# Where split weights stand in their buffers: one fixed place, or 64 places in turn

## The chip, the cores and the metric

One Trainium2 chip, of which the kernel uses one core. The metric is device time in microseconds (us) of one execution of the whole program; smaller is better. Times of several executions are given as a median with the lowest and the highest.

## What is computed

One step of a decoder layer for a prompt group (256 tokens) and a sample group (8 sequences of 4 tokens), served with the same weights. With D_MODEL = 2048 and D_FF = 8192, the reference comes down to

```python
h = rms_norm(x, g_mix)
u_lin, u_gate, q_sb, k_sb, v_sb, q_mem, gate_logits = split(h @ w_in)
y_conv = silu(layer_norm(depthwise_causal_conv(u_lin * sigmoid(u_gate)))) @ w_conv_out
y_sb   = stick_breaking_attention(rms_norm(q_sb), rms_norm(k_sb), v_sb) @ w_sb_out
y_mem  = softmax_attention(rms_norm(q_mem), mem_k, mem_v) @ w_mem_out
g      = sigmoid(gate_logits + b_gate)            # three gates of D_MODEL each
x = x + (g[0]*y_conv + g[1]*y_sb + g[2]*y_mem) @ w_o
x = x + square(relu(rms_norm(x, g_mlp) @ w_up)) @ w_down
```

All data are float32. Keys, values and convolution history are returned as well. Nearly all of the arithmetic is in the products with the weight matrices, which are some 264 MB and are each used for all 288 tokens at once.

## The kernel before, in words

**Precision.** A float32 product is made of three products in the one-pass type F32R. Each operand is split into a high part (a rounded copy) and a low part (what is left), and weight and activation are multiplied as high by high, high by low and low by high.

**Slabs.** All weights lie in `wall`, cut in the order of use into 504 slabs of 128 partitions by 1,024 numbers (`SLAB`), that is, 8 blocks of 128 by 128. For each slab four steps follow each other:

1. SP issues the load into one of four `wr` buffers (`load_slab`, the DMA on L283).
2. ScalarE casts it to the high part, in one of four `wh` buffers (`cast_weights`, L305).
3. VectorE subtracts, which gives the low part, in one of four `wl` buffers (`sub_part`, L316).
4. TensorE uses it: `products` (L494) makes 24 matmuls out of a full slab, 8 blocks by three products, all issued by `chunk` on L488.

In each matmul on L488 the stationary operand (the weights that TensorE loads) is a block of 128 columns of a `wh` or `wl` buffer. The moving operand is an activation tile of 288 columns, and the result is added up in a PSUM bank.

**The first 16 slabs** (for the memory's keys and values, `mem_products`) are used the other way round: the slab is the moving operand, 512 columns at a time, and a block of an activation is the stationary one (L541). They are loaded and split in two halves of 512.

**Places.** `wh` and `wl` tiles have 1,088 numbers in a partition, 64 (`PAD`) more than a slab needs. `shifted` (L286 to L288) returns the part of such a tile that begins at a given number of elements:

```python
    def shifted(p, s):
        n = 0 if s < 2 * KT // 2 else SHIFT
        return tl(p, [P, SLAB + PAD], F32R)[:, n:n + SLAB]
```

`KT` is 16, so slabs 0 to 15 begin at 0 and slabs 16 to 503 at `SHIFT`, which is 5. L305 and L316 write the part that it returned and L488 reads blocks of it.

The moving tiles have places of their own. The class `Acts` (L325) takes tiles of 320 numbers (`APART`) from the pool `a` and begins 4 (`AHEAD`) in, or 32 for the memory's tokens. `make_homes` (L1243) cuts buffers of the pools `k4` and `s` into tiles that begin 36 (`HOME`) in, or 36 plus a multiple of 320. By the addresses of the built program, counted in 4-byte words modulo 64, this comes to the following: every moving tile of L488 begins at word 60, every block of weights on L488 at word 29, and on L541 both operands at word 24. Of the small products with operands of their own, L853 to L855 (attention scores and values, 256 columns or 128) have stationary operands at word 56 and moving ones at 56 or 24, and L827 (sums of squares for a head, 288 columns, stationary operand `ones_r`) has them at 8 and at 24 or 56. L1107 to L1109 and L908 are transposes.

**Order.** The order of the work is made by a small planner in the kernel (the class `Order`), with a generator for each job and estimated costs. It decides on each engine what comes next from those costs, buffers that come free, and ranks. The place of a slab enters none of its numbers.

Of the kernel before, what the change touches and what calls it, by code (L numbers as in the profile page):

```python
# [16 lines left out]
KT = D_MODEL // P  # L17
# [156 lines left out]
APART = 320  # L174
AHEAD, HOME = 4, 36
PAD = 64
SHIFT = 5
VISIT, VISIT_K = 4, 8
MM = 0.131
MM_MEM = 0.226  # L180
# [3 lines left out]
def tile_decoder_step(ctx: ExitStack, tc: tile.TileContext, xT, memT, wall, cvec, kmat, ptab,  # L184
# [23 lines left out]
    def tl(p, shape, dt=F32):  # L208
        cnt[0] += 1
        return pools[p].tile(shape, dt, tag=p, name=f"{p}_{cnt[0]}")  # L210
# [73 lines left out]
        sl.landed[part].at = order.landed(n * P * 4 / 1e3)  # L284

    def shifted(p, s):  # L286
        n = 0 if s < 2 * KT // 2 else SHIFT
        return tl(p, [P, SLAB + PAD], F32R)[:, n:n + SLAB]  # L288

    def due(s):  # L290
# [4 lines left out]
    def cast_weights():  # L295
        todo = [(0, 0), (1, 0), (0, 1), (1, 1)] + [(s, i) for s in range(2, N_SLABS) for i in range(slabs[s].parts)]
        for s, i in todo:
            sl = slabs[s]
            n = SLAB // sl.parts
            cast_at[0] = s  # L300
            yield act(n, sl.landed[i], **({} if i else {"w": 1}))
            if i == 0:
                sl.h = shifted("wh", s)
            c = slice(i * n, (i + 1) * n)
            nc.scalar.copy(sl.h[:, c], sl.raw[:, c])  # L305
            sl.split[i].cast = order.now.ready
            add(sub_part(s, i), lambda s=s: 0 if due(s) - order.free["DVE"] < 5.0 else 4.5)

    def sub_part(s, i):
        sl = slabs[s]  # L310
        n = SLAB // sl.parts
        yield dve(n, late=Order.HOP + 0.1)
        if i == 0:
            sl.l = shifted("wl", s)
        c = slice(i * n, (i + 1) * n)
        nc.vector.tensor_sub(sl.l[:, c], sl.raw[:, c], sl.h[:, c].bitcast(F32))  # L316
        done(sl.split[i])
        if i == sl.parts - 1:
            give("wr")
# [1301 lines left out]
```

## Time and profile before

| what | value |
| --- | --- |
| median of 2 runs | 1635.16 us (1635.15 to 1635.18) |
| profiled execution, span from first to last instruction | 1632.5 us |
| TensorE busy, share of the span | 1627.7 us, 100% |
| VectorE busy | 992.1 us, 61% |
| ScalarE busy | 739.3 us, 45% |
| GpSimd busy | 139.1 us, 9% |
| HBM read, written | 297.05 MB, 6.32 MB |
| matmuls | 12,786, of which 11,712 on L488 |

The profiled execution's own time is its span, 1632.5 us, and what lies around it: the median of the runs is 2.7 us more than the span. Rows name an engine (PE is TensorE's matmuls, PEld its weight loads, DVE VectorE, ACT ScalarE, POOL GpSimd, SP the queue that issues DMAs), a line of the kernel, an operation, and tiles as result<-operands. "Who waited for whom" gives idle time of an engine by what ended it. The chain of waits is followed back from the last instruction, and shows what the end of the program hangs on; its pieces have a start, a length, a line and a count. In the windows each engine's busy time stands for a stretch of time, with the granted TensorE clock as a share of full speed. Matmuls overlap each other, so the time that a stream of them takes is read from the distance of their starts, not from the busy time of one.

### The profile page before, as it was taken

To read this page: it belongs to the slowest core of one execution; us is meant where nothing else is said; L and a number is where in the kernel's file an instruction comes from. 1 tells how busy PE (TensorE), PEld (TensorE's weight loads), DVE (VectorE), ACT (ScalarE), POOL (GpSimd) and SP (SyncE) were. 2 spreads that over 40 slices of the span, in tenths; PEclk is the share of its full clock that TensorE was granted. 3 is DMA by queue.
4 is the path that set the end of the run, shared out by engine and by line. 5 is a ranking of instruction groups with operands and counts; after the bars stand their busy time and mean duration, and the time that the engine had idled before them with its cause. 6 is when DMAs were issued, how large, how long until landed. Compare 5 with 4: busy or idle time off the path is not lost.

```text
span 1632.5 us, 30962 instructions
## 1 busy us (share of the span) xinstructions
PE 1627.7 (100%) x12786; PEld 1610.3 (99%) x12786; DVE 992.1 (61%) x1471; ACT 739.3 (45%) x1070; POOL 139.1 (9%) x104
## 2 busy tenths in 40 slices
PE   9999999999999999999999999999999999999999
PEld 7999999999999999999999999999999999999999
DVE  8889888877677655565555544455445554455443
ACT  8746766644444534444443333333333333333332
POOL 0020000000000000001222200121001210022100
PEclk9999999999999999999999999999999999999999
DMA  9787465777755555546655555555555555555563
GB/s 339 217 186 251 153 209 189 248 257 252 254 166 169 163 179 167 174 153 212 191 176 168 169 168 168 169 169 174 165 173 170 168 170 169 168 168 168 180 194 99
DMA packets 107103, 305.39 MB, mean 187 GB/s; under 512 B 19922, under 2 KB 29522, under 8 KB 106962
## 3 DMA queue, kind: packets, MB, share of 16 engines
q1 hardware_dynamic: 106818, 303.39, 58.2%
q8 instruction: 100, 1.64, 0.4%
q14 instruction: 41, 0.34, 0.1%
q10 hardware_dynamic: 144, 0.02, 0.0%
HBM read 297.05 MB, written 6.32 MB: 186 GB/s over the span
## 4 chain that ended last, share of the span: by engine, by line
PE 99%; DMA 0%; SPq 0%; ACT 0%; DVE 0%; issue 0%
PE pm L488 93%; PE pm L541 3%; PE pa L488 1%; PE pl L1017 1%; PE pl L1190 0%; PE pa L854 0%; PE pa L855 0%; PE pa L853 0%; DMA wr<-in_wall 0%; PE pl L1033 0%; PE pa L827 0%; PE pa L1144 0%; PE pa L908 0%; PE pa L1141 0%; PE pa L1143 0%; PE pa L1107 0%
## 5 line engine op out<-in xcount | busy, mean ns | idle before, releaser
L305 ACT CAST wh<-wr 128x1024 fp32r<-128x1024 f32 (+1 forms) x520 | 530.3, 1022 | 648.1 <-PE pm L488 597.0
L488 PE MATMUL pm<-a,wh 128*128 128x288 f32 x5184 | 739.1, 293 | 0.0
L316 DVE TENSOR_TENSOR wl<-wr,wh 128x1024 fp32r<-128x1024 f32 (+1 forms) x520 | 617.2, 1190 | 195.2 <-ACT wh L305 190.5
L488 PEld LDWEIGHTS pm<-a,wh 128*128 128x128 f32 x5184 | 696.7, 188 | 1.3 <-issue 1.2
L488 PE MATMUL pm<-a,wl 128*128 128x288 f32 x2592 | 397.0, 292 | 0.0
L488 PEld LDWEIGHTS pm<-a,wl 128*128 128x128 f32 x2592 | 358.4, 188 | 0.0
L488 PE MATMUL pm<-k,wh 128*128 128x288 f32 x2160 | 306.7, 292 | 0.0
L488 PEld LDWEIGHTS pm<-k,wh 128*128 128x128 f32 x2160 | 290.2, 188 | 0.0
L488 PE MATMUL pm<-k,wl 128*128 128x288 f32 x1120 | 171.6, 292 | 0.0
L488 PEld LDWEIGHTS pm<-k,wl 128*128 128x128 f32 x1120 | 155.1, 188 | 0.0
L1346 POOL TENSOR_TENSOR t<-t 128x288 f32<-128x288 f32 x64 | 96.7, 1511 | 599.5 <-DVE t L1343 599.5
L1360 DVE TENSOR_TENSOR a<-a,pm 128x288 f32<-128x288 f32 x64 | 29.0, 454 | 122.4 <-PE pm L488 122.4
L1343 DVE SCALAR_TENSOR_TENSOR t<-pm,rx 128x288 f32<-128x288 f32 x64 | 29.2, 457 | 90.4 <-PE pm L488 90.4
L1349 ACT CAST k<-t 128x288 fp32r<-128x288 f32 x56 | 24.1, 433 | 115.6 <-POOL t L1346 115.6
L1262 DVE TENSOR_TENSOR t<-pm,rx 128x288 f32<-128x288 f32 x48 | 22.0, 458 | 71.5 <-PE pm L488 71.5
L488 PE MATMUL pm<-s,wh 128*128 128x288 f32 x400 | 65.1, 292 | 0.0
L719 DVE SCALAR_TENSOR_TENSOR a<-a,cv,a 128x256 f32<-128x256 f32 x120 | 57.5, 480 | 1.4
L1332 POOL TENSOR_TENSOR t<-t,t 128x288 f32<-128x288 f32 x15 | 21.6, 1441 | 419.3 <-ACT t L1329 419.3
L488 PEld LDWEIGHTS pm<-s,wh 128*128 128x128 f32 x400 | 56.6, 188 | 0.0
L1351 DVE TENSOR_TENSOR k<-t,k 128x288 fp32r<-128x288 f32 x52 | 23.8, 458 | 51.1 <-ACT k L1349 51.1
L541 PE MATMUL pm<-wh,a 128*128 128x512 f32 x128 | 34.6, 391 | 0.2 <-ACT wh L305 0.2
L488 PE MATMUL pm<-s,wl 128*128 128x288 f32 x160 | 33.8, 292 | 0.0
(212 smaller groups left out, 784.4 us busy)
## 6 DMA issues: line engine op xcount, KB each, us to landing
wr<-in_wall SPq DMA_DIRECT2D x488, 512.0 KB, 3.6
wr<-in_wall SPq DMA_DIRECT2D x32, 256.0 KB, 4.8
k<-in_kpool SPq DMA_DIRECT2D x32, 256.0 KB, 5.9
k<-in_vpool SPq DMA_DIRECT2D x32, 256.0 KB, 5.8
k<-in_mkc SPq DMA_DIRECT2D x8, 512.0 KB, 10.2
k<-in_mvc SPq DMA_DIRECT2D x8, 512.0 KB, 6.5
t<-in_xT SPq DMA_DIRECT2D x16, 144.0 KB, 3.7
out_yT<-a SPq DMA_DIRECT2D x16, 144.0 KB, 1.9
```

What stands on the lines that cost most here:

```text
L305: nc.scalar.copy(sl.h[:, c], sl.raw[:, c])
L316: nc.vector.tensor_sub(sl.l[:, c], sl.raw[:, c], sl.h[:, c].bitcast(F32))
L488: nc.tensor.matmul(ps, w, a, start=(first and i == 0), stop=(last and i == len(todo) - 1))
L541: nc.tensor.matmul(ps[m], y[:, m * P:(m + 1) * P], z[:, w], start=(k == 0 and j < 2), stop=(k == KT - 1 and j in (4, 5)))
L719: nc.vector.scalar_tensor_tensor(c[:, :NP], up[:, k:k + NP], w, c[:, :NP], op0=ALU.mult, op1=ALU.add)
L1262: nc.vector.tensor_mul(g, ps, rx)
L1332: nc.gpsimd.tensor_add(sq_sum[0], sq_sum[0], res[0])
L1343: nc.vector.scalar_tensor_tensor(r, ps, 0.0, r2, op0=ALU.max, op1=ALU.mult)
L1346: nc.gpsimd.tensor_mul(r, r, r)
L1349: nc.scalar.copy(a.h, r)
L1351: nc.vector.tensor_sub(a.l, r, a.h.bitcast(F32))
L1360: nc.vector.tensor_add(x1[j], x1[j], ps)
```

## The change

The constant 5 goes, and a slab's place is worked out from its number instead: slabs 16 to 19 begin at 4, slabs 20 to 23 at 5, and so on up to 63, then again from 0; the last slab, 503, begins at 61. Slabs 0 to 15 stay at 0. In words modulo 64, the blocks of weights on L488 now begin at each of the 64 words in turn, with 96 matmuls at each before the next one, most words twice over the program. The moving operands stay at word 60.

```diff
 PAD = 64
-SHIFT = 5
+RUN = 4
 VISIT, VISIT_K = 4, 8
...
     def shifted(p, s):
-        n = 0 if s < 2 * KT // 2 else SHIFT
+        n = 0 if s < 2 * KT // 2 else s // RUN % PAD
         return tl(p, [P, SLAB + PAD], F32R)[:, n:n + SLAB]
```

The instructions of the built program are the same before and after, in the same order on each of the five engines, with the same shapes and buffers. Only the addresses inside the `wh` and `wl` buffers differ.

## The prediction

> **What bounds the kernel now.** I read three views in this order: who TensorE waited for, the chain of waits by time, and the windows. The first shows whether TensorE ever stands still. Its columns are us in total, times, longest:
>
> ```profile
> PE pa L1409 <- POOL eps L234: 1.3, 1, 1.3
> PE pm L541 <- ACT wh L305: 0.2, 1, 0.2
> ```
>
> After its first matmul it waits 1.5 us in 1632.5. The chain is therefore TensorE's own stream; its long pieces (start us, us, line, matmuls) are
>
> ```profile
> 439.90 79.43 PE pm L488 x611
> ...
> 541.70 297.18 PE pm L488 x2286
> ...
> 839.15 790.15 PE pm L488 x6078
> ```
>
> Divide: 79.43/611, 297.18/2286 and 790.15/6078 all give 130.0 ns from one matmul to the next. I call that time the pitch. It is the same whichever buffers are in turn and whatever ScalarE, VectorE and the DMAs do beside it: the windows below (stretch, length, busy us and count of PE, PEld, DVE, ACT, POOL, granted clock, DMA share, GB/s) go from a VectorE that is 61% busy to one that is 49% busy, and the clock is granted in full throughout.
>
> ```profile
> 440.00:840.00 400.00, 400.00 (x3079) 400.00 (x3078) 245.19 (x353) 181.99 (x239) 21.61 (x15) 1.00 0.56 175
> 1040.00:1440.00 400.00, 400.00 (x3079) 400.00 (x3079) 195.87 (x225) 145.18 (x161) 48.54 (x32) 1.00 0.54 170
> ```
>
> Busy time of a single matmul (about 292 ns in the groups) is no price here, since matmuls overlap; only the pitch is. The matmuls of L488 that the change can touch are counted from the answer on that line:
>
> ```profile
> L488 PE MATMUL pm<-a,wh x5184: 289/292/401, 54.0 to 1528.1; 128*128 128x288 f32 x200
> L488 PE MATMUL pm<-a,wl x2592: 289/292/383, 54.6 to 1529.2; 128*128 128x288 f32 x200
> L488 PE MATMUL pm<-k,wh x2160: 290/290/294, 730.3 to 1627.3; 128*128 128x288 f32 x197
> L488 PE MATMUL pm<-k,wl x1120: 290/292/294, 732.4 to 1628.7; 128*128 128x288 f32 x187
> L488 PE MATMUL pm<-s,wh x400: 290/294/294, 734.8 to 1628.0; 128*128 128x288 f32 x134
> L488 PE MATMUL pm<-s,wl x160: 290/290/294, 736.3 to 1629.0; 128*128 128x288 f32 x160
> L488 PE MATMUL pa<-a,wh x64: 290/292/382, 48.9 to 72.8; 128*128 128x288 f32 x64
> L488 PE MATMUL pa<-a,wl x32: 290/293/298, 49.4 to 73.1; 128*128 128x288 f32 x32
> ```
>
> They sum to 11,712, which is 488 slabs by 24. At 130.0 ns they are 1522.6 us, 93% of the span. So the time is 11,712 pitches plus about 110 us that the change cannot reach, and 1 ns on every pitch is 11.7 us, 0.72%. Two per cent of the time, which is about what a measurement of this kernel can tell from no change, is 2.8 ns of pitch.
>
> **The change part by part.** No instruction is added, removed or moved on any engine, and none has another shape. What moves are addresses. Counted in 4-byte words and modulo 64, every moving operand of L488 starts at word 60, before and after. Every stationary operand starts at word 29 before; after, it runs through all 64 words, four slabs (96 matmuls) on each, nearly two rounds over the 488 slabs. Three things touch these addresses.
>
> *ScalarE's cast and VectorE's subtraction* write the slab at the new places. Before already has two places: the first 16 slabs are split in halves of 512 at place 0, the others whole at place 5.
>
> ```profile
> L316 DVE TENSOR_TENSOR wl<-wr,wh 128x1024 fp32r<-128x1024 f32 x488 | 596.1, 1223 | 192.9 <-ACT wh L305 188.4 <-ACT t L1329 1.5 <-DMA wr<-in_wall 1.3
> L305 ACT CAST wh<-wr 128x1024 fp32r<-128x1024 f32 x488 | 511.8, 1049 | 645.0 <-PE pm L488 597.0 <-issue 25.9 <-DMA wr<-in_wall 9.6
> L1349 ACT CAST k<-t 128x288 fp32r<-128x288 f32 x56 | 24.1, 433 | 115.6 <-POOL t L1346 115.6
> L1351 DVE TENSOR_TENSOR k<-t,k 128x288 fp32r<-128x288 f32 x52 | 23.8, 458 | 51.1 <-ACT k L1349 51.1
> L316 DVE TENSOR_TENSOR wl<-wr,wh 128x512 fp32r<-128x512 f32 x32 | 21.1, 688 | 2.3 <-ACT wh L305 2.1
> L305 ACT CAST wh<-wr 128x512 fp32r<-128x512 f32 x32 | 18.6, 614 | 3.1 <-DMA wr<-in_wall 2.9
> ```
>
> The lines through 288 and 1024 elements give 433 + 224 x (1049 - 433)/736 = 620 ns for a cast of 512 and 458 + 224 x (1223 - 458)/736 = 691 ns for a subtraction. Measured at place 0 are 614 and 688. Within 1% the place has no price there. I take nothing. The cover is TensorE's time on a slab, 24 x 130.0 = 3.12 us, against 1.05 and 1.22 us on two engines; the cast itself idles 597.0 us waiting for TensorE to free a buffer. If the cover were gone TensorE would wait at each slab for what exceeds 3.12 us, so both would have to grow more than twofold before anything is paid.
>
> *The weight load.* Where the moving operand is short, TensorE goes at the pace of the loads. Transposes of 128 columns and ordinary products of 256 columns stand in the chain as follows:
>
> ```profile
> 142.14 0.12 PE pa L853
> 142.25 0.12 PE pa L854
> 142.37 0.12 PE pa L855
> 142.49 0.12 PE pa L853
> 142.61 0.12 PE pa L854
> 142.73 0.12 PE pa L855
> 142.85 3.14 PE pm L488 x24
> 145.99 0.12 PE pa L853
> ...
> 146.70 0.79 PE pm L488 x6
> ...
> 153.75 0.11 PE pa L1107
> 153.86 0.11 PE pa L1108
> 153.97 0.11 PE pa L1109
> 154.07 0.44 PE pa L908 x4
> ```
>
> Three 128-column steps take 154.07 - 153.75 = 0.32 us, 107 ns each. A load thus has 130 - 107 = 23 ns to spare under a matmul of L488. A load that a bad place lengthens by less than that costs nothing by itself. What could cost is that the load and the moving stream, which both read SBUF at once, get into each other's way.
>
> *The pitch against the distance between the two operands.* No L488 matmul has another place, so this is bounded from neighbours. The six products of 256 columns from 142.14 have their stationary operands at word 56 and the moving ones at word 24, a distance of 32; the six from 145.99 have both at 56, a distance of 0. Both groups take 0.71 us, 118.3 ns each, so these two distances are alike to about 2 ns. The first stage (512 columns, both operands at word 24, distance 0) shows in the timeline of TensorE:
>
> ```profile
> 20.35 1.07 PE L541 MATMUL pm<-wh,a 128*128 128x512 f32 x4
> 21.25 0.61 PE L541 MATMUL pm<-wl,a 128*128 128x512 f32 x2
> 21.71 1.07 PE L541 MATMUL pm<-wh,a 128*128 128x512 f32 x4
> 22.61 0.61 PE L541 MATMUL pm<-wl,a 128*128 128x512 f32 x2
> 23.07 1.07 PE L541 MATMUL pm<-wh,a 128*128 128x512 f32 x4
> ```
>
> Twelve steps from 20.35 to 23.07 are 226.7 ns each. The straight line through these two groups, (226.7 - 118.3)/256 = 0.423 ns per column, puts 288 columns at 118.3 + 32 x 0.423 = 131.9 ns. L488, whose operands lie 31 words apart, takes 130.0. So the nearest rows with other places are 1.9 ns dearer than before's. That is the only sign in the trace that place matters, and it is weak: length, line and place change together, and a distance of 32, next to L488's 31, is among the dearer ones, so if it is place at all, a word or two already makes the difference.
>
> The bounds: at the low end, 288 columns at 0.423 ns are 121.9 ns, so if the whole fixed part of a pitch vanished the gain would be 8.1 ns, 95 us. No row of the trace lies near that. At the high end stand the lone 288-column products with `ones_r` at word 8:
>
> ```profile
> 132.80 0.14 PE pa L827
> 132.94 5.48 PE pm L488 x42
> ...
> 140.42 0.14 PE pa L827
> 140.56 1.58 PE pm L488 x12
> ```
>
> They take 140 ns, 10 ns more, which would be 117 us if all of it were place; but they are single matmuls behind a wait and into another bank, so most of that need not be place. Between these ends I go by the nearest rows, 0 to 1.9 ns. Since the 64 places hold before's own as well as those unlike it, evenly, I take half, 1.0 ns, as the mean over all of them.
>
> The sum: 11,712 x 1.0 ns = 11.7 us on the span of 1632.5, giving 1644.2. The median of the runs, 1635.16, stands 2.7 us above the span for what lies around it. Forecast: **1647 us**, 0.7% slower.
>
> **A rule against this.** The trace first: pitch is 130.0 in every long piece, while the cast and the subtraction write neighbouring buffers. The Trainium skill, TensorE: Matmul & The Clock Gate, section on what happens when one issues a matmul, says that TensorE has two independent read ports, so that loading the next weights takes no read bandwidth from the running matmul. By that rule no distance between operands can matter and the sum would be 1635. The constant pitch agrees but does not test it, since all of these rows have one distance; it is the first rival.
>
> **The rivals.**
>
> *The place has no price, and the time stays (not slower).* The mechanism: the pitch is the stream of 288 columns plus a fixed step, and the load with 23 ns to spare hides whatever a place does to it. For it: the pitch does not move by 0.1 ns in 1,000 us. Against it: the 1.9 ns above. The time is 1635.2, and it decides if the mean pitch after stays under 130.2.
>
> *Bad places are much worse than the rows show.* If the two reads meet in the same part of the memory, some places could cost what L827 shows. With half of the places at 10 ns the mean is 5 ns, 58.6 us: 1694. For it: L827's rows and that nothing in before tests the other 63 places. Against it: distances 0 and 32 in the 256-column products differ by no more than 2 ns.
>
> *Word 29 is itself a bad place.* Then an even mix is faster: the mirror of my own price, 1.0 ns, gives 1623; for 2% it would need 2.8 ns. Against it: L488 lies below the line through the other lengths, not above.
>
> *The change does nothing that it says.* The first 16 slabs keep place 0, but the built program does have stationary operands at all 64 words, so I give this no chance of its own.
>
> **How the numbers follow.** Forecast, slower by between 0.2% and 2%: 0.42. No price: 0.33. Much worse, over 2%: 0.21. Faster: 0.04, half of it over 2%. Within 2% are the forecast, the flat case and half the faster one, 0.77; slower by over 2% 0.21; faster by over 2% 0.02. The range has to hold the flat case, so it starts just under it, at 1633; at the top it goes to 1690, 4.7 ns of mean pitch, leaving out the worse half of the second rival. The forecast's own range is 1638 to 1667.
>
> **What would show it.** In the chain after, the long pieces of L488 should no longer divide to one value: stretches of 96 matmuls should differ, with the same values again 256 slabs later, and the mean over the piece of some 6,078 should be about 131.0 (796 us instead of 790.15). TensorE's waits should stay near 1.5 us, and the cast and subtraction at 1049 and 1223 ns; if either has grown and TensorE waits for it, the cost was not in the pitch. A pitch of 130.0 at every place proves the first rival; a few places at 140 and more, the second; places under 128, the third. What would make the prediction wrong in kind is a pitch that depends on something other than the place, such as a clock granted below 1.00.

## The result, and the profile after

| | before | after |
| --- | --- | --- |
| median of 2 runs | 1635.16 us (1635.15 to 1635.18) | 1659.33 us (1659.16 to 1659.5) |
| span of the profiled execution | 1632.5 us | 1657.4 us |
| mean pitch on L488 (11,637 steps from one of its matmuls to the next) | 130.3 ns | 132.4 ns |

The change makes the kernel slower: the ratio of the times is 1.0148, with a 95% interval of 1.0119 to 1.0178, so it is 1.5% slower, which is under two per cent but clear of no change. That is 24 us where 12 were forecast. The sign and the mechanism, a dearer pitch, were as predicted; the size was not.

TensorE waits as little as before, and the granted clock is 1.00 in the profile of this and of every other run below. Who it waited for, in us, times and longest:

```profile
PE pa L1409 <- POOL eps L234: 1.3, 1, 1.3
```

The cast and the subtraction of a slab take what they took (1049 and 1223 ns before), although they now write at 64 places. The columns are busy us and the mean ns of one, then the idle time before them:

```profile
L316 DVE TENSOR_TENSOR wl<-wr,wh 128x1024 fp32r<-128x1024 f32 x488 | 595.6, 1222 | 199.2 <-ACT wh L305 195.9 <-ACT t L1329 1.6 <-ACT s L226 0.6
...
L305 ACT CAST wh<-wr 128x1024 fp32r<-128x1024 f32 x488 | 511.2, 1048 | 667.0 <-PE pm L488 615.7 <-issue 29.8 <-DMA wr<-in_wall 9.2
```

The chain of waits is still TensorE alone. Its long pieces after 440 us (start us, us, line, matmuls):

```profile
525.40 22.26 PE pm L488 x168
547.66 0.13 PE pa L443
547.80 0.14 PE pa L444
547.93 303.27 PE pm L488 x2286
851.21 0.13 PE pa L443
851.34 0.13 PE pa L444
851.47 802.69 PE pm L488 x6078
```

The same 2,286 and 6,078 matmuls took 297.18 and 790.15 us before: 6.1 and 12.5 us more. Of the 24.9 us on the span the other 6.2 lie ahead of these pieces' start (547.93 against 541.70 us). The pieces divide to 132.7 and 132.1 ns, but they are no longer of one kind. Asked for 10 us inside one place each, the chain answers, for words 5, 11, 15 and 23 in turn:

```profile
626.90 10.16 PE pm L488 x76
```
```profile
702.93 10.07 PE pm L488 x74
```
```profile
753.94 10.14 PE pm L488 x78
```
```profile
854.93 10.15 PE pm L488 x78
```

Divide each: 133.7, 136.1, 130.0 and 130.1 ns. By the starts of all matmuls in the trace, taken over the 96 of each place the second time it comes up (the only time, for words 22 to 27), 13 of the 64 words have a pitch within 0.3 ns of 130.0, the value of before. 24 words lie between 133.0 and 133.5, 25 between these groups, and words 5 and 11 lie above, at 133.9 and 136.0. None is under 129.9.

Within a place the pitch repeats with a short period. At word 15 it goes 132, 128, 132, 128; at word 11 it goes 140, 140, 131, 139, 130 and starts again. I call that a rhythm. 31 words come up twice after 440 us, where no other matmuls cut into the stretches but a few; 29 of them have the same mean both times to 0.5 ns. Words 1 and 56 do not: word 56 has 130.0 ns the first time and 131.7 the second.

### The profile page after: what moved, and what is told of

It reads as the page before. It is cut to its first block, busy times and chain, and to the rows that moved or that the text cites. A ratio compares the mean times of both kernels' runs of the same rounds, so it can differ in the third digit from the quotient of the medians.

```text
span 1657.4 us, 30962 instructions
## 1 busy us (share of the span) xinstructions
PE 1652.8 (100%) x12786; PEld 1635.6 (99%) x12786; DVE 992.2 (60%) x1471; ACT 738.5 (45%) x1070; POOL 138.3 (8%) x104
## 4 chain that ended last, share of the span: by engine, by line
PE 100%; POOL 0%; DVE 0%; issue 0%; POOLq 0%
PE pm L488 93%; PE pm L541 3%; PE pa L488 1%; PE pl L1017 1%; PE pl L1190 0%; PE pa L854 0%; PE pa L855 0%; PE pa L853 0%; PE pl L1033 0%; PE pa L1409 0%; PE pa L827 0%; PE pa L1144 0%; PE pa L908 0%; PE pa L1141 0%; PE pa L1143 0%; PE pa L1107 0%
## 5 line engine op out<-in xcount | busy, mean ns | idle before, releaser
L488 PE MATMUL pm<-a,wh 128*128 128x288 f32 x5184 | 749.9, 295 | 0.0
L488 PEld LDWEIGHTS pm<-a,wh 128*128 128x128 f32 x5184 | 706.4, 188 | 1.3 <-issue 1.2
L488 PE MATMUL pm<-a,wl 128*128 128x288 f32 x2592 | 402.5, 295 | 0.0
L488 PEld LDWEIGHTS pm<-a,wl 128*128 128x128 f32 x2592 | 362.8, 188 | 0.0
L488 PE MATMUL pm<-k,wh 128*128 128x288 f32 x2160 | 311.3, 295 | 0.0
L488 PEld LDWEIGHTS pm<-k,wh 128*128 128x128 f32 x2160 | 294.2, 188 | 0.0
L488 PE MATMUL pm<-k,wl 128*128 128x288 f32 x1120 | 173.9, 295 | 0.0
L488 PEld LDWEIGHTS pm<-k,wl 128*128 128x128 f32 x1120 | 156.9, 188 | 0.0
L1349 ACT CAST k<-t 128x288 fp32r<-128x288 f32 x56 | 24.2, 433 | 116.6 <-POOL t L1346 116.6
L488 PE MATMUL pm<-s,wh 128*128 128x288 f32 x400 | 65.9, 295 | 0.0
L488 PEld LDWEIGHTS pm<-s,wh 128*128 128x128 f32 x400 | 57.4, 188 | 0.0
L488 PE MATMUL pm<-s,wl 128*128 128x288 f32 x160 | 34.1, 294 | 0.0
```

Of the source, the lines that this page charges most:

```text
L488: nc.tensor.matmul(ps, w, a, start=(first and i == 0), stop=(last and i == len(todo) - 1))
L1349: nc.scalar.copy(a.h, r)
```

## The experiments

Letters stand for theories throughout. A: where the weights begin sets the pitch, by their own word (A1) or by the distance to the moving operand (A2, or A2' if the memory repeats after fewer words). B: changing the place costs, not the place. C and D were formed on the way.

**Place or change of place.** Two kernels: one fixed place at the dearest word, and the change with eight places that had been cheap.

```diff
-SHIFT = 5
+SHIFT = 51
```

> The kernel before with its one fixed place moved, SHIFT 51 for 5: every block of weights on L488 begins at word 11 modulo 64, the dearest word in the changed kernel's trace (136.0 ns from matmul to matmul there, 130.0 at word 29). Theory A, the pitch depends on where the weights begin (by their own word, or by the distance to the moving operand): 11,712 x 6.0 ns = 70 us more, a span of 1702.8 and a time of 1705. Theory B, what costs is changing the place every four slabs: no change is left, so 1635.

```diff
+GOOD = (55, 63, 0, 3, 5, 7, 23, 39)
...
-        n = 0 if s < 2 * KT // 2 else s // RUN % PAD
+        n = 0 if s < 2 * KT // 2 else GOOD[s // RUN % 8]
```

> A new place with every fourth slab as in the change, but only eight places in turn, those whose pitch was 130.0 to 130.1 ns in the changed kernel's trace: words 15, 23, 24, 27, 29, 31, 47 and 63. Theory A: 1635. Theory B: as many changes of place as in the change, so 1659.

Word 11 alone took 1662.69 us beside 1635.19 for the kernel before: a fixed place is slower without any change of place, so B is not all of it, but 27.5 us are not the 70 of theory A. The chain of that kernel shows why:

```profile
443.67 83.39 PE pm L488 x636
527.06 0.13 PE pa L443
527.19 0.13 PE pa L444
527.32 22.03 PE pm L488 x168
549.35 0.13 PE pa L443
549.48 0.13 PE pa L444
549.62 310.89 PE pm L488 x2286
860.51 0.14 PE pa L443
860.64 0.14 PE pa L444
860.78 796.91 PE pm L488 x6078
```

131.1, 131.1, 136.0 and 131.1 ns. The weights never leave word 11, and yet there are two rhythms. Each holds for hundreds of microseconds, and the steps from one to the other fall on the second and the third passage of the products on L443 and L444 after 440 us, a quarter of a microsecond of other work (the first passage changes nothing). A change of buffers makes no step: the moving tiles of pool `k4` come in at 746.9 us, in the middle of the 136.0 piece. The eight cheap places took 1646.47 us, between the two forecasts. Words 15, 24, 29, 31 and 63 kept 130.0 there; word 27, 130.0 in the changed kernel, had mostly 134.9 (10.12 us for 75 steps in the row below), word 23 132.2 and word 47 131.7:

```profile
899.00 10.12 PE pm L489 x75
```

From this came **theory C**: a pair of places has one or more steady rhythms, and which of them is entered depends on what ran just before.

**Own word or distance.** The moving operands were shifted, once with all 64 places of the weights, once with the weights fixed at word 29.

```diff
-AHEAD, HOME = 4, 36
+AHEAD, HOME = 24, 56
```

> The changed kernel with all moving operands of L488 20 words further on (AHEAD 24, HOME 56): they begin at word 16 instead of 60, and the weights run through all 64 words as in the change. Theory A1, a weight block's own word counts: the same pitch by word as in the change (29 at 130.0, 11 at 136.0), mean 132.35, time 1659. Theory A2, only the distance between the two operands counts: the list of pitches moves by 20 words, so that word 31 has the 136.0 of word 11, word 29 the 131.7 of word 9, and words 35, 43, 47, 49 and 51 have 130.0; mean and time again about 132.35 and 1659.

```diff
-AHEAD, HOME = 4, 36
+AHEAD, HOME = 22, 54
```

> The kernel before, weights at word 29 as before, but the moving operands at word 14 (AHEAD 22, HOME 54), so that the distance between the two is that of the dearest place, 49 words. Theory A1, the weights' own word counts: 130.0 ns, time 1635. Theory A2, the distance counts: 136.0 ns, 70 us more, time 1705.

Both theories failed. With the weights at word 29, untouched, and only the moving operands elsewhere, the time was 1673.27 us:

```profile
552.76 304.81 PE pm L488 x2286
...
857.84 804.27 PE pm L488 x6032
```

This is 133.3 ns in both pieces: not the 130.0 of A1, not the 136.0 of A2. So the moving operand's place counts too, though the weights have not moved. The distance alone does not give the pitch either, unless it has a third rhythm besides the 131.1 and 136.0 of word 11; the lists of the runs below decide that. The other run (1666.28 us) gave a list of 64 pitches that agrees with the change's neither as it stands nor moved by 20 words: the largest correlation over all 64 shifts is 0.24, though it is at 20. 20 is no multiple of 8, which matters below.

**How far both can move together.** Shifts of the moving operands by 16, 8 and 1 words, with the weights at all places.

```diff
-AHEAD, HOME = 4, 36
+AHEAD, HOME = 20, 52
```

> The changed kernel with all moving operands of L488 16 words further on (AHEAD 20, HOME 52), at word 12 instead of 60; weights at all 64 words in turn. The run with the moving operands 20 words on gave a list of pitches that was neither the list of the change nor that list moved by 20. Theory A2' (the memory repeats every 16 words, so that moving both operands by 16 changes nothing): the list moves by 16 words, and words 31, 39, 40, 43, 45 and 63 have 130.0. Theory C (a pair of words has its own set of steady rhythms, and there is no simple shift): no likeness at any shift. By both the mean is 131.5 to 133 and the time 1649 to 1667.

```diff
-AHEAD, HOME = 4, 36
+AHEAD, HOME = 12, 44
```

> The changed kernel with the moving operands 8 words further on (AHEAD 12, HOME 44), at word 4. If the pieces have 8 words: the list of the change moved by 8, word by word, as it did for 16. If they have 16 words: no likeness at any shift. Mean and time as in the others, 131.5 to 133 ns and 1649 to 1667.

```diff
-AHEAD, HOME = 4, 36
+AHEAD, HOME = 5, 37
```

> The changed kernel with all moving operands of L488 one word further on (AHEAD 5, HOME 37), at word 61. With 16 words the list of pitches moved by exactly 16, with 20 it did not move but became another. Theory D (the chip's memory is read in pieces of 16 words, or of 8; within a piece the start of the moving operand counts too): no likeness at a shift of 1 nor anywhere; floor again at 130.0, since it has been there in all lists; mean 131.5 to 133. If only the distance counted after all: the list moved by 1, with 130.0 at words 16, 24, 25, 28, 30, 32, 48 and 0.

The times were 1658.27, 1659.2 and 1695.13 us. Here are some entries of the lists (second time round), each with the weights moved as far as the moving operand, so that a row has one distance:

| weights, moving at 60 | as in the change | both +8 | both +16 | both +20 | both +1 |
| --- | --- | --- | --- | --- | --- |
| word 11 | 135.98 | 135.97 | 135.97 | 136.38 | 133.31 |
| word 15 | 130.07 | 130.02 | 130.07 | 133.27 | 136.64 |
| word 29 | 130.01 | 130.00 | 130.01 | 133.27 | 136.64 |
| word 31 | 130.09 | 130.09 | 130.09 | 132.52 | 133.50 |
| word 38 | 133.36 | 133.38 | 133.36 | 130.05 | 136.64 |
| all 64: largest difference | | 0.05 | 0.09 | 4.52 | 8.88 |

Moving both by 8 or by 16 words changes nothing at any of the 64 places; by 20 it changes 46 of them by more than 0.5 ns, by 1 it changes 58. The chain shows it for word 11 of the change (74 steps in 10.07 us) at word 19 with both moved by 8, and at word 27 with both moved by 16; in each, 10.20 us for 75 steps, 136.0 ns:

```profile
804.43 10.20 PE pm L488 x75
```
```profile
905.90 10.20 PE pm L488 x75
```

So the pitch depends on the distance of the two operands and on where the moving one starts modulo 8 words (32 bytes). A smaller number would not do: of the numbers that divide 8 all but 8 itself divide 20 as well, and a shift by 20 is not without effect. That is theory D of the expectation above, with 8 for its piece; A2' had 16. In the three runs that agree the moving operands begin at words 60, 4 and 12, which are all 4 modulo 8; for other starts no run repeats a list. The run with the moving operands one word on shows what else lies there:

```profile
558.84 309.05 PE pm L488 x2286
...
868.15 821.94 PE pm L488 x6078
```

That is 135.2 ns over these 8,364 matmuls. In the list of the second time round no word is below 131.6, and word 41 is at 140.0. The floor of 130.0, which I expected to return, is gone.

**The number of changes.** A new place with every slab:

```diff
-RUN = 4
+RUN = 1
```

> The change with RUN 1 for 4: a new place with every slab, 487 changes of place instead of 121, and every word as often as in the change. Theory B' (each change has a cost of its own; the 24.9 us of the change over 121 changes are 0.2 us each): 487 x 0.2 = 100 us, a time of 1735. Theory C (the place sets what rhythms there are, a change only picks one): a mean near 132.35 ns as in the change, 1659, within 8 us.

It took 1658.15 us: four times as many changes of place, and 1.2 us less than the change. Its last long piece:

```profile
850.94 802.17 PE pm L488 x6078
```

Theory B, a cost of each change, is out. By the starts of its matmuls, word 11 has 131.0 ns here each of the six times after 440 us, and had 136.0 both times in the change, though word 10 runs before it in both kernels. Its two rhythms thus show without L443 and L444 as well, and the place just before is not all that picks one: word 10 ran for 24 matmuls here and for 96 in the change.

**History.** Five places that had shown only the floor, and word 27 alone:

```diff
+GOOD = (55, 0, 5, 7, 39)
...
-        n = 0 if s < 2 * KT // 2 else s // RUN % PAD
+        n = 0 if s < 2 * KT // 2 else GOOD[s // RUN % 5]
```

> A new place with every fourth slab, but only the five words at which every stretch had 130.0 ns after 440 us, in the change and in the run with eight words: 15, 24, 29, 31 and 63. Theory B': 121 changes as in the change, 1659. Theory C: these words have no other rhythm that a change could pick, so 1635 to 1638.

```diff
-SHIFT = 5
+SHIFT = 3
```

> The kernel before with all weights at word 27 (SHIFT 3). The change had 130.0 ns at this word, both times that it came to it; the run with eight words had 134.9 there nearly every time. Theory A (one price for a word): one of the two throughout, so 1635 or 1692, the same in every execution. Theory C (two steady rhythms, picked by what came before): long stretches at one value, with a step only where other matmuls come between (L443 and L444, or the small products of the first 440 us); a time anywhere from 1635 to 1692, and executions may differ by more than the 0.02 us of the kernel before.

The five places took 1642.16 us, more than the 1638 that theory C allowed. Four words behaved. Word 63 had 130.0 behind words 62 and 47 in the earlier runs; behind word 31 it fell into 133.3 nearly every time (10.13 us for 76 steps), with an exception soon after a passage of L443 and L444 (10.14 us for 78 steps, 130.0 ns):

```profile
671.89 10.13 PE pm L489 x76
```
```profile
859.94 10.14 PE pm L489 x78
```

So my list of words with one rhythm was too short a test, and theory C stands with one more word of two rhythms. Word 27 alone took 1691.45 us (four runs, 1691.40 to 1691.51), 1.0347 times the kernel before (1.033 to 1.0364):

```profile
448.02 85.86 PE pm L488 x636
...
557.09 308.60 PE pm L488 x2286
...
865.96 820.53 PE pm L488 x6078
```

135.0 ns in each piece, past L443 and L444 without a step, and the four times agree to 0.11 us. The step between pieces that theory C expected did not come. What remains of it is the comparison: the same pair of words has 130.0 ns in the changed kernel and 135.0 here, so there is no one price for a word. After 440 us the change comes to word 27 once, and not twice as the expectation says: slabs 12 to 15, the first that would fall on it, stay at 0.

**Who reads, who writes.** The place was split: written as before, read by TensorE at word 11.

```diff
+    def read_at(w, c0):
+        c0 += 46 if c0 == 0 else -18
+        return w[:, c0:c0 + P]
...
-            chunk(ps, [(w[:, c:c + P], a.l if x else a.h) for w, c, a, x in part],
+            chunk(ps, [(read_at(w, c), a.l if x else a.h) for w, c, a, x in part],
...
-            chunk(ps[o], [(w[:, c], getattr(hx[k], x)) for w, c, x, k in todo], k2 == 0, k2 == KT // 2 - 1)
+            chunk(ps[o], [(read_at(w, c.start), getattr(hx[k], x)) for w, c, x, k in todo], k2 == 0, k2 == KT // 2 - 1)
```

> The kernel before, whose casts and subtractions still write at place 5, word 29; but the matmuls on L488 read their blocks 18 words lower (46 higher for the first block), so that every block of weights begins at word 11 for TensorE alone. The products are therefore of shifted columns of the weights: this leaves the reference's values, and keeps every instruction, shape and wait. If TensorE's own reading sets the pitch: the two rhythms of the run with the weights at word 11, 131.1 and 136.0 ns, and a time near its 1663, anywhere from 1648 to 1705. If it is where ScalarE and VectorE write: 130.0 and 1635.

1662.67 us, against 1662.69 when the writes were at word 11 too, with the pieces the same to the last digit (the lines below L485 stand four further down in this kernel):

```profile
443.63 83.39 PE pm L492 x636
...
527.29 22.03 PE pm L492 x168
...
549.58 310.89 PE pm L492 x2286
...
860.75 796.91 PE pm L492 x6078
```

Where ScalarE and VectorE write the weights plays no part here; where TensorE reads them does.

## Why the prediction was wrong in size

*What bounds the kernel, and the count.* Right. The time is 11,712 pitches and a rest that hardly moved: 11,637 steps that are 2.08 ns longer make 24.2 of the 24.9 us on the span. TensorE waits no more than before.

*Cast and subtraction at no price.* Right: 1048 and 1222 ns at 64 places.

*The price of a pitch.* This step failed, in its last sentence. The line through 256 and 512 columns put other places 1.9 ns above before's, and that was near the mean (132.4 - 130.3 = 2.1 ns). Then I took half of it, "since the 64 places hold before's own as well as those unlike it, evenly". They do not hold them evenly: 13 words of 64 are at the floor and 51 are not, so before's place was one of a few good ones and not one end of a scale. The term was 11.7 us and measured 24. Without the halving the sum would have come near, but that may be luck: in the rows behind the 1.9 ns length, line and place change together, and no run shows that their line holds for places alone. One remark beside it was right: a word or two makes the difference, since words 28 and 30 have 133.2 and 133.4 ns beside the 130.0 of word 29.

*Distance as the variable.* Wrong, though the sum did not need it. I compared the rows by the distance between the operands, and found 31 and 32 words unlike. The run with the weights left at word 29 (1673 us) and the shifts by 20 and by 1 show that the start of the moving operand modulo 8 words counts as well.

*The rule of two read ports.* The Trainium skill, TensorE: Matmul & The Clock Gate, section on what happens when one issues a matmul, says that loading weights does not take read bandwidth from the running matmul. By that rule, as I read it, the time would have stayed at 1635. The runs disagree with this: with the same instructions and no wait added, the places of the two operands move the pitch from 130.0 to as much as 140.0 ns. Whether it is read bandwidth that the two take from each other is not shown.

*The rivals.* The flat one is out. The much worse one did not come in the change: the worst mean of a place there is 6.0 ns, at one word, and 24 of the 51 bad words cost 3.0 to 3.5. Its mean of 5 ns came in two other kernels, with all weights at word 27 (1691 us) and with the moving operands one word further on (1695 us). That word 29 is a bad place is out: no list has a pitch below 129.9.

*The signs to look for.* Different values by stretches of 96 came, and a mean of 132.1 in the last piece where 131.0 was forecast. The same values 256 slabs later came for 29 of the 31 words that can be compared. The forecast did not think of two rhythms for one pair of places: word 27 ran at 130.0 ns in the change and at 135.0 by itself.

What stays open is how the two reads disturb each other inside the chip. No row shows a read of the memory; that the places of both operands count, that it is TensorE's reading for the weights, and that 8 words are the unit for moving operands that start at 4 modulo 8 is shown. How the reads meet, why a rhythm lasts, and whether the place at which the moving operands are written counts, is not.

None of these places beats the kernel before: no list has a pitch below 129.9 ns, and before has 130.0 throughout after 440 us.

## What to carry to other kernels

Where TensorE runs a stream of equal matmuls without a wait, read the pitch from long pieces of the chain (time by count), and treat the start addresses of both operands as a setting that can cost per cents: here 0 to 8% of a pitch, with no instruction changed. When one such setting is at the floor, keep both operands at their places modulo 8 words and keep their distance, in every buffer that takes turns; these runs show that for shifts of 8 and 16 words. To average over places is not a middle way when most places are bad, as 51 of 64 are here.

## What was not expected of the hardware

A steady stream of matmuls can have two speeds at the same places modulo 64 words, and keeps the one that it has for long: at word 11, 131.1 ns for 636 and 168 matmuls, then 136.0 for 2,286, then 131.1 for 6,078, with two foreign matmuls at each step between the unlike pieces. And the unit is small: 8 words of 4 bytes. Both operands moved by that much give the same 64 pitches to within 0.05 ns, while one word more for the moving operand alone costs the whole program 36 us over the change.
